# Two paired row blocks of five up tiles as seven block products instead of eight, with the loads of x spaced out

## The chip, the cores and the metric

The kernel runs on one core of a Trainium2 chip. The metric is the time of one execution in device microseconds (us), as the median of several runs. PE is TensorE (matmuls), PEld its weight loads, DVE is VectorE, ACT ScalarE, POOL GpSimd, and SP the engine whose queue issues most loads.

## The reference, cut to what matters

One layer of an encoder block in float32: 256 tokens (T), width 2048 (D, 16 row blocks of 128), feed-forward width 5632. Two attention mixers come first; then

```
gu = rms_norm(h, norm_pre_ffn) @ w_gate_up        # (256, 2048) x (2048, 11264)
g, up = gu[..., :5632], gu[..., 5632:]
h = h + rms_norm((silu(g) * up) @ w_down, norm_post_ffn)
```

The very first product, at the other place that the change touches, makes the latents: `u @ w_in` for the columns of q_lat (768) and kv_lat (512), where u is the normalised x.

## The kernel before, in words

**Products in three matmuls.** Every float32 product A B is done with A = Ah + Al and B = Bh + Bl, each half rounded to the matmul's float32r type: Ah Bh + Al Bh + Ah Bl. ACT makes the high half (a copy), DVE the low half (a subtraction), from raw weights that SP's queue loads. All this is one unit: a raw tile of 128 x 1024 (512 KB), and its hi and lo tiles. There are four buffers each of raw, hi and lo.

**The up product** (`up`, `two_products`, `up_unit`, line 805 on) goes over 11 tiles c. A tile makes 512 columns of g (side j = 0) and 512 of up (j = 1) for two token halves t of 128. For each of the 16 row blocks k there is one unit, and for each t and j three matmuls (lines 688 to 690) with 128 x 128 tokens as the stationary operand and 512 weight columns moving: 12 per unit, 192 per tile. The sums of (t, j) stand in PSUM: two buffers of two banks (`mm_pair`), one for each t. The first two units and the last two are ordered token half by token half, so that t = 0 ends 12 matmuls ahead of t = 1. `up_out` then makes silu(g) on ACT (line 861) and its product with up on DVE (line 863, tile ht); only then may the next tile write that buffer. Two units later PE transposes ht (`turn_split`, line 706) into one of four further banks (`at_bank`), from which ACT and DVE split it (lines 709, 710) into hid, which the down product reads.

**The first product** (`first_products`) goes over the 16 blocks k of x and, for each, three pairs p of latent blocks of q: 96 pairs of one 512 wide and one 256 wide matmul. Each k needs a block of x (`load_x`, `split_x`) and a unit of weights. Blocks 0 to 3 of x are loaded on SP's queue; after unit k, for k = 0 to 5, ACT's queue issues the load of blocks 2k + 4 and 2k + 5. When a pair of latents is done, its PSUM halves are added (lines 381, 382), one half j at a time with one tile tb for both; the kv product reuses the banks of the first pair.

**Order.** The kernel is written in Tile: a planner puts each engine's instructions into one order at build time, taking earlier lines of the program first among those that it reckons ready. Each engine then runs its list strictly in that order and waits at semaphores.

Of the kernel before, what the change touches and what calls it, by code (L numbers as in the profile page):

```python
# [10 lines left out]
F32 = mybir.dt.float32  # L11
# [3 lines left out]
ALU = mybir.AluOpType  # L15
# [39 lines left out]
def block_kernel(ctx: ExitStack, tc: tile.TileContext, a: dict, out: bass.AP):  # L55
# [11 lines left out]
    def slot(name, dt=F32):  # L67
        return sl.tile([P, 2, T], dt, tag="slot", name=name)
# [43 lines left out]
    def load_x(queue, k, n):  # L112
        if k % 2 == 0:
            xT[k // 2] = slot(f"xT{k // 2}")
        return queue.dma_start(xT[k // 2][:, k % 2:k % 2 + n], a["xT"][:, k:k + n, :]).ins

# [218 lines left out]
    def first_products():  # L335
# [7 lines left out]
        for k, p in order:  # L343
            if k not in w:
                if k < 3:
                    loaded = load_x(nc.sync, k, 1 if k < 2 else 2)
                with ExitStack() as held:
                    for ins in split_ins if k else ():
                        held.enter_context(tc.issue_after(ins.ins))
                    xsplit = split_x(k)  # L350
                with tc.issue_after(loaded), tc.issue_after(xsplit):
                    w[k] = unit("w_lat", 768, (256, 768) if k < 3 else None, (256, 768) if k == 0 else None)
                if 2 * k + 4 < KD:
                    with tc.issue_after(split_ins[0].ins):
                        load_x(S, 2 * k + 4, 2)
            hi, lo = w[k]
# [7 lines left out]
            if k == KD - 1:  # L364
                yield ps[p]

# [4 lines left out]
    for nm, n in (("q", 6), ("kv", 4)):  # L371
        acc = slot(f"acc_{nm}")[:, 0]
        g = cols[f"{nm}_norm"]
        for p in range(n // 2):
            s = tmp.tile([P, 2, T], F32, tag="t2", name="s", bufs=6)
            if nm == "kv":
                fold(pair(f"lat_{nm}{p}", "w_lat", KD, 4, xk), None, s)
            else:
                tb = tmp.tile([P, 2, T], F32, tag="t2", name="tb", bufs=6)
                for j, half in enumerate(next(q_products)):  # L380
                    S.activation(tb[:, j], half[:, T:], AF.Copy)
                    V.tensor_tensor(s[:, j], half[:, 0:T], tb[:, j], op=ALU.add)
            sq = tmp.tile([P, 2, T], F32, tag="t2", name="sq", bufs=6)
# [185 lines left out]
    def flat(t):  # L569
        return t.rearrange("p a b -> p (a b)")  # L570
# [230 lines left out]
    for t in range(2):  # L801
        for n in range(4):
            mg[t, n] = flat(slot(f"mg{t}{n}"))
    ahead = [[[flat(slot(f"{nm}_w_gu{k}{j}", F32R)) for j in range(2)] for nm in ("hi", "lo")] for k in range(AHEAD)]
    def up_unit(c, k):

        off = streams.get("w_gu", 0)
        streams["w_gu"] = off + P * 1024
        src = a["w_gu"][off:off + P * 1024].rearrange("(p c) -> p c", p=P)
        raw = wp.tile([P, 1024], F32, tag="raw", name=f"raw_w_gu_{off}", bufs=4)  # L810
        nc.sync.dma_start(raw, src)
        g = gf[:, k:k + 1]
# [46 lines left out]
    def up_out(ps, t, hts):  # L859
        s = tmp.tile([P, 512], F32, tag="t2", name="s", bufs=6)  # L860
        S.activation(s, ps[:, 0], AF.Silu, scale=r2s[t])
        ht = tmp.tile([P, 512], F32, tag="t2", name="ht", bufs=6)
        V.scalar_tensor_tensor(ht, ps[:, 1], r2s[t], s, op0=ALU.mult, op1=ALU.mult)  # L863
        hts.append(ht)

    def up(c):
# [17 lines left out]
    for c in range(KF // 4):  # L884
        up(c)

# [112 lines left out]
```

## Time and profile before

| | us |
|---|---|
| median of 3 runs (1383.34 to 1384.69) | 1383.67 |
| the profiled execution's own time | 1384.21 |
| its span, first to last instruction | 1382.5 |
| PE busy / DVE busy / ACT busy in the span | 1374.2 / 794.4 / 681.1 |

Busy time is what instructions took by their records; pipelined instructions of one engine overlap a little, so starts are the better measure of the pace. The own time of the profiled execution is 1.7 us more than the span, and 0.54 us more than the median.

### The profile page before, as it was taken

To read this page: it belongs to the slowest core of one execution; us is meant where nothing else is said; L and a number is where in the kernel's file an instruction comes from. 1 tells how busy PE (TensorE), PEld (TensorE's weight loads), DVE (VectorE), ACT (ScalarE), POOL (GpSimd) and SP (SyncE) were. 2 spreads that over 40 slices of the span, in tenths; PEclk is the share of its full clock that TensorE was granted. 3 is DMA by queue.
4 is the path that set the end of the run, shared out by engine and by line. 5 is a ranking of instruction groups with operands and counts; after the bars stand their busy time and mean duration, and the time that the engine had idled before them with its cause. 6 is when DMAs were issued, how large, how long until landed. Compare 5 with 4: busy or idle time off the path is not lost.

```text
span 1382.5 us, 16825 instructions
## 1 busy us (share of the span) xinstructions
PE 1374.2 (99%) x6414; PEld 1143.6 (83%) x6414; DVE 794.4 (57%) x921; ACT 681.1 (49%) x823; POOL 59.1 (4%) x95
## 2 busy tenths in 40 slices
PE   9999999999999999999999999999999999999998
PEld 8888888888888888888888888888888888888886
DVE  7996866555545566666545554555555545444444
ACT  6654444466558444555544444444444453434343
POOL 3310000000003100000000000000000001000000
PEclk9999999999999999999999999999999999999999
DMA  8655654565567655673666656565665666666663
GB/s 258 206 186 177 194 165 152 157 186 185 173 206 262 209 184 182 208 236 109 189 193 191 184 182 198 185 193 185 185 196 186 190 204 209 188 197 196 190 192 121
DMA packets 74545, 262.35 MB, mean 190 GB/s; under 512 B 8545, under 2 KB 9057, under 8 KB 74337
## 3 DMA queue, kind: packets, MB, share of 16 engines
q1 hardware_dynamic: 71424, 253.00, 58.8%
q0 software_dynamic: 1744, 6.29, 1.3%
q10 hardware_dynamic: 1296, 1.99, 0.4%
q8 instruction: 50, 0.82, 0.2%
q14 instruction: 31, 0.25, 0.0%
HBM read 259.15 MB, written 2.10 MB: 189 GB/s over the span
## 4 chain that ended last, share of the span: by engine, by line
PE 98%; DVE 1%; ACT 0%; issue 0%
PE gu_ps L688 12%; PE gu_ps L690 12%; PE gu_ps L689 12%; PE wd_ps L213 6%; PE wd_ps L215 6%; PE wd_ps L214 6%; PE gate_ps L213 4%; PE gate_ps L215 4%; PE gate_ps L214 4%; PE q_sb_ps L177 2%; PE k_sb_ps L177 2%; PE wout_ps L213 2%; PE wo_ps L690 2%; PE wout_ps L214 2%; PE wo_ps L688 2%; PE wo_ps L689 2%
## 5 line engine op out<-in xcount | busy, mean ns | idle before, releaser
L824 DVE SCALAR_TENSOR_TENSOR lo_w_gu<-raw_w_gu,packed,hi_w_gu 128x1024 fp32r<-128x1024 f32 x172 | 220.8, 1284 | 210.5 <-ACT hi_w_gu L823 208.9
L823 ACT ACTIVATE hi_w_gu<-raw_w_gu,packed 128x1024 fp32r<-128x1024 f32 x172 | 198.2, 1152 | 231.6 <-PE gu_ps L689 231.0
L688 PE MATMUL gu_ps<-hi_w_gu,hs 128*128 128x512 f32 x704 | 276.6, 393 | 0.0
L690 PE MATMUL gu_ps<-lo_w_gu,hs 128*128 128x512 f32 x704 | 275.3, 391 | 0.0
L689 PE MATMUL gu_ps<-hi_w_gu,hs 128*128 128x512 f32 x704 | 274.3, 390 | 0.0
L105 DVE TENSOR_TENSOR lo_w_down<-raw_w_down,hi_w_down 128x1024 fp32r<-128x1024 f32 x88 | 111.1, 1264 | 118.6 <-ACT hi_w_down L104 118.5
L104 ACT ACTIVATE hi_w_down<-raw_w_down 128x1024 fp32r<-128x1024 f32 x88 | 93.2, 1061 | 135.6 <-PE wd_ps L214 127.4
L688 PEld LDWEIGHTS gu_ps<-hi_w_gu,hs 128*128 128x128 f32 x704 | 132.2, 188 | 28.6 <-DVE ht L863 2.3
L690 PEld LDWEIGHTS gu_ps<-lo_w_gu,hs 128*128 128x128 f32 x704 | 132.2, 188 | 27.4
L689 PEld LDWEIGHTS gu_ps<-hi_w_gu,hs 128*128 128x128 f32 x704 | 132.2, 188 | 27.3 <-DVE hs L792 0.3
L105 DVE TENSOR_TENSOR lo_w_gate<-raw_w_gate,hi_w_gate 128x1024 fp32r<-128x1024 f32 x64 | 79.1, 1240 | 70.5 <-ACT hi_w_gate L104 64.3
L213 PE MATMUL gate_ps<-hi_w_gate,xs 128*128 128x512 f32 x256 | 100.6, 393 | 0.0
L215 PE MATMUL gate_ps<-lo_w_gate,xs 128*128 128x512 f32 x256 | 99.8, 390 | 0.0
L214 PE MATMUL gate_ps<-hi_w_gate,xs 128*128 128x512 f32 x256 | 99.6, 389 | 0.0
L104 ACT ACTIVATE hi_w_gate<-raw_w_gate 128x1024 fp32r<-128x1024 f32 x64 | 67.4, 1055 | 62.5 <-PE gate_ps L214 52.1
L104 ACT ACTIVATE hi_w_o<-raw_w_o 128x1024 fp32r<-128x1024 f32 x32 | 34.0, 1061 | 51.4 <-PE wo_ps L689 45.2
L105 DVE TENSOR_TENSOR lo_w_out<-raw_w_out,hi_w_out 128x1024 fp32r<-128x1024 f32 x32 | 39.2, 1225 | 33.6 <-ACT hi_w_out L104 33.4
L105 DVE TENSOR_TENSOR lo_w_o<-raw_w_o,hi_w_o 128x1024 fp32r<-128x1024 f32 x32 | 39.2, 1224 | 31.3 <-ACT hi_w_o L104 30.8
L215 PEld LDWEIGHTS gate_ps<-lo_w_gate,xs 128*128 128x128 f32 x256 | 48.1, 188 | 10.2
L214 PEld LDWEIGHTS gate_ps<-hi_w_gate,xs 128*128 128x128 f32 x256 | 48.1, 188 | 9.6
L213 PEld LDWEIGHTS gate_ps<-hi_w_gate,xs 128*128 128x128 f32 x256 | 48.1, 188 | 9.6
L104 ACT ACTIVATE hi_w_out<-raw_w_out 128x1024 fp32r<-128x1024 f32 x32 | 34.0, 1062 | 42.2 <-PE wout_ps L214 27.7
(452 smaller groups left out, 2541.8 us busy)
## 6 DMA issues: line engine op xcount, KB each, us to landing
raw_w_gu<-in_w_gu SPq DMA_DIRECT2D x176, 512.0 KB, 3.5
raw_w_down<-in_w_down SPq DMA_DIRECT2D x88, 512.0 KB, 4.2
raw_w_gate<-in_w_gate SPq DMA_DIRECT2D x64, 512.0 KB, 3.6
raw_w_o<-in_w_o SPq DMA_DIRECT2D x32, 512.0 KB, 3.7
raw_w_out<-in_w_out SPq DMA_DIRECT2D x32, 512.0 KB, 4.2
raw_w_q<-in_w_q SPq DMA_DIRECT2D x16, 512.0 KB, 3.8
raw_w_k<-in_w_k SPq DMA_DIRECT2D x16, 512.0 KB, 3.6
raw_w_v<-in_w_v SPq DMA_DIRECT2D x16, 512.0 KB, 3.5
```

The lines of the kernel that those rows point to most:

```text
L104: split_ins[0] = S.activation(hi[:, cs], raw[:, cs], AF.Copy)
L105: split_ins[1] = V.tensor_tensor(lo[:, cs], raw[:, cs], hi[:, cs].bitcast(F32), op=ALU.subtract)
L177: TE.matmul(ps[:, j, :], lhsT=hi[:, o:o + P], rhs=r, start=k == 0, stop=False, skip_group_check=True)
L213: TE.matmul(ps[t], lhsT=l[0][:, ts], rhs=hi[:, cs], start=k == 0, stop=False)
L214: TE.matmul(ps[t], lhsT=l[1][:, ts], rhs=hi[:, cs], start=False, stop=False)
L215: mm = TE.matmul(ps[t], lhsT=l[0][:, ts], rhs=lo[:, cs], start=False, stop=k == K - 1)
L688: TE.matmul(ps[t][:, j], lhsT=x[0][:, ts], rhs=hi[j], start=k == 0, stop=False)
L689: TE.matmul(ps[t][:, j], lhsT=x[1][:, ts], rhs=hi[j], start=False, stop=False)
L690: mm = TE.matmul(ps[t][:, j], lhsT=x[0][:, ts], rhs=lo[j], start=False, stop=k == K - 1)
L823: split_ins[0] = S.activation(hi, raw, AF.Copy, scale=g)
L824: split_ins[1] = V.scalar_tensor_tensor(lo, raw, g, hi.bitcast(F32), op0=ALU.mult, op1=ALU.subtract)
```

## The change

**Up tiles c = 1 to 5** run `up_fast`. In them the row blocks 8 and 10 form a pair, and 9 and 11 another. Before, a pair cost 2 blocks x 2 token halves x 2 sides = 8 products of a 128 x 128 by a 128 x 512 block, of three matmuls each. Now it costs seven (the scheme of Strassen in Winograd's form): 21 matmuls for 24.

- `token_sums`, once, makes the four sums of token blocks that the scheme needs, for both pairs, and splits them.
- `fast_pair` loads both raw units, lets ACT scale them in place by the norm's gain, and makes seven blocks of 128 x 512 from them, each split by a copy on ACT and a subtraction on DVE: three are as loaded, one (t3) is a difference of two of these, and three (T1, T2, T4) are a chain of differences in which each is made from the one before. The halves stand in tiles of the pool `sl`, not in the four hi and lo buffers.
- Three of the seven products go straight into the tile's PSUM sums. Four go to four banks of their own (q), over both pairs. They use all of `at_bank`'s four.
- At the step "collect", after the second pair, ACT copies one of the four banks and DVE makes four additions; at the end of the tile DVE adds the result to each of the four PSUM sums (four more), into SBUF tiles, on which `up_out` then works in place.
- The units of a tile stand in the order 0 to 3, pair, 4 to 7, pair, 12 to 15.

**The first product.** Blocks 4 and 5 of x are loaded after unit 0 as before, then blocks k + 3 and k + 4 after the units k = 3, 5, 7, 9, 11. Each load of two blocks is one contiguous stretch of memory. The first two pairs of latents are folded as whole pairs (`fold`); the third still goes by halves, with a tile tb for each.

```diff
+PAIRS = ((8, 10), (9, 11))
+FAST = range(1, 6)
...
-                if 2 * k + 4 < KD:
+                if k == 0 or k % 2 == 1 and 3 <= k < KD - 4:
                     with tc.issue_after(split_ins[0].ins):
-                        load_x(S, 2 * k + 4, 2)
+                        load_x(S, k + 3 if k else 4, 2)
...
             if k == KD - 1:
-                yield ps[p]
+                yield both[p] if p < 2 else ps[p]
...
+            elif p < 2:
+                fold(next(q_products), None, s)
             else:
-                tb = tmp.tile([P, 2, T], F32, tag="t2", name="tb", bufs=6)
                 for j, half in enumerate(next(q_products)):
-                    S.activation(tb[:, j], half[:, T:], AF.Copy)
-                    V.tensor_tensor(s[:, j], half[:, 0:T], tb[:, j], op=ALU.add)
+                    tb = tmp.tile([P, T], F32, tag="t2", name="tb", bufs=6)
+                    S.activation(tb, half[:, T:], AF.Copy)
+                    V.tensor_tensor(s[:, j], half[:, 0:T], tb, op=ALU.add)
...
     def up_out(ps, t, hts):
...
+        own = isinstance(ps, list)
+        gate, lin = ps if own else (ps[:, 0], ps[:, 1])
+        s = gate if own else tmp.tile([P, 512], F32, tag="t2", name="s", bufs=6)
+        S.activation(s, gate, AF.Silu, scale=r2s[t])
+        ht = lin if own else tmp.tile([P, 512], F32, tag="t2", name="ht", bufs=6)
+        V.scalar_tensor_tensor(ht, lin, r2s[t], s, op0=ALU.mult, op1=ALU.mult)
         hts.append(ht)
...
+    def token_sums():
...
+        def whole(o, k, t):
+            V.tensor_tensor(o, hs[:, k, 0, t].bitcast(F32), hs[:, k, 1, t].bitcast(F32), op=ALU.add)
...
+        V.tensor_tensor(s1, a21, a22, op=ALU.add)
+        V.tensor_tensor(s2, s1, a11, op=ALU.subtract)
+        V.tensor_tensor(s3, a11, a21, op=ALU.subtract)
+        V.tensor_tensor(s4, a12, s2, op=ALU.subtract)
...
+    def split_part(x, name):
+        hi, lo = flat(slot(f"{name}h", F32R)), flat(slot(f"{name}l", F32R))
+        split_ins[0] = S.activation(hi, x, AF.Copy)
+        split_ins[1] = V.tensor_tensor(lo, x, hi.bitcast(F32), op=ALU.subtract)
+        return hi, lo
...
+    def fast_pair(c, p, ps, q):
...
+        ra, rb = up_raw(c, ka), up_raw(c, kb)
+        for r, k in ((ra, ka), (rb, kb)):
+            S.activation(r, r, AF.Copy, scale=gf[:, k:k + 1])
+        (b11, b12), (b21, b22) = two_sides(ra), two_sides(rb)
...
+        product(q[0], rows(ka, 0), split_part(b11, f"fb11{c}{p}"), **ends)
+        product(ps[0][:, 0], rows(kb, 0), split_part(b21, f"fb21{c}{p}"))
+        product(ps[0][:, 1], sums[3, p], split_part(b22, f"fb22{c}{p}"))
+        t3 = flat(slot(f"ft3{c}{p}"))
+        V.tensor_tensor(t3, b22, b12, op=ALU.subtract)
+        V.tensor_tensor(b12, b12, b11, op=ALU.subtract)
+        product(q[3], sums[0, p], split_part(b12, f"ft1{c}{p}"), **ends)
+        product(q[2], sums[2, p], split_part(t3, f"fu3{c}{p}"), **ends)
+        V.tensor_tensor(b22, b22, b12, op=ALU.subtract)
+        product(q[1], sums[1, p], split_part(b22, f"ft2{c}{p}"), **ends)
+        V.tensor_tensor(b21, b21, b22, op=ALU.subtract)
+        return product(ps[1][:, 0], rows(kb, 1), split_part(b21, f"ft4{c}{p}"))
...
+        order = [(k, t) for t in range(2) for k in range(HEAD)] + [(2, 0), (2, 1), (3, 0), (3, 1), "pair0"]
+        order += [(k, t) for k in range(4, 8) for t in range(2)] + ["pair1", "collect"]
+        order += [(k, t) for k in (12, 13) for t in range(2)] + [(k, t) for t in range(2) for k in (14, 15)]
...
+            if step == "collect":
+                q1 = tmp.tile([P, 512], F32, tag="t2", name="q1", bufs=6)
+                S.activation(q1, q[0], AF.Copy)
+                add = [tmp.tile([P, 512], F32, tag="t2", name=f"q{i}", bufs=6) for i in range(3)]
+                V.tensor_tensor(add[0], q[1], q1, op=ALU.add)
+                V.tensor_tensor(add[1], q[2], add[0], op=ALU.add)
+                V.tensor_tensor(add[0], q[3], add[0], op=ALU.add)
+                V.tensor_tensor(add[2], q[3], add[1], op=ALU.add)
+                add = [[q1, add[0]], [add[1], add[2]]]
...
+            if k == KD - 1:
+                for j in range(2):
+                    V.tensor_tensor(add[t][j], ps[t][:, j], add[t][j], op=ALU.add)
+                up_out(add[t], t, hts)
...
-        up(c)
+        up_fast(c) if c in FAST else up(c)
```

## Rows read from the trace of the kernel before

**Rows 1.** The profile page of the whole execution: its first part (busy time of each engine and share of the span) and the engine sums of the chain that ended last.

```profile
PE 1374.2 (99%) x6414; PEld 1143.6 (83%) x6414; DVE 794.4 (57%) x921; ACT 681.1 (49%) x823; POOL 59.1 (4%) x95
...
PE 98%; DVE 1%; ACT 0%; issue 0%
```

**Rows 2.** All waits of PE over the whole span: waiter, line <- what released it: us in total, times, longest.

```profile
PE last L907 <- ACT diag L906: 1.7, 1, 1.7
PE warm L369 <- DVE ones L85: 1.1, 1, 1.1
PE lat_kv_ps L177 <- DVE s L382: 0.8, 1, 0.8
```

**Rows 3.** Waits from 660 to 1160 us, which holds the tiles c = 1 to 10 of the up product; same columns.

```profile
ACT hi_w_gu L823 <- PE gu_ps L689: 230.4, 166, 2.9
DVE lo_w_gu L824 <- ACT hi_w_gu L823: 208.9, 148, 2.7
...
PEld gu_ps L688 <- DVE ht L863: 2.3, 9, 0.3
```

**Rows 4.** Busy time of each engine in a stretch as long as one up tile (window, its length, then us busy and instructions of PE, PEld, DVE, ACT, POOL, granted clock, DMA share, GB/s).

```profile
730.15:774.75 44.60, 44.60 (x201) 36.74 (x200) 23.17 (x20) 20.65 (x21) 0.00 (x0) 1.00 0.61 189
```

**Rows 5.** Timeline of PE near the end of the tile c = 1 (start, us, engine, line, operation): two matmuls that stand twelve apart, and the first transposes of its hid. The tile's last matmul starts at about 732.2.

```profile
726.74 0.39 PE L688 MATMUL gu_ps<-hi_w_gu,hs 128*128 128x512 f32 x1
...
729.46 0.39 PE L688 MATMUL gu_ps<-hi_w_gu,hs 128*128 128x512 f32 x1
...
738.22 0.60 PE L706 MATMUL hid<-ident,ht 128*128 128x128 f32 x4
```

**Rows 6.** The page's costliest groups, those of the up tiles (busy us in all, mean ns of one | idle before them).

```profile
L824 DVE SCALAR_TENSOR_TENSOR lo_w_gu<-raw_w_gu,packed,hi_w_gu 128x1024 fp32r<-128x1024 f32 x172 | 220.8, 1284 | 210.5 <-ACT hi_w_gu L823 208.9
L823 ACT ACTIVATE hi_w_gu<-raw_w_gu,packed 128x1024 fp32r<-128x1024 f32 x172 | 198.2, 1152 | 231.6 <-PE gu_ps L689 231.0
...
L688 PEld LDWEIGHTS gu_ps<-hi_w_gu,hs 128*128 128x128 f32 x704 | 132.2, 188 | 28.6 <-DVE ht L863 2.3
```

**Rows 7.** Instructions that write or read the tile hid, for c = 1: shortest/median/longest ns, first and last start.

```profile
L709 ACT ACTIVATE hid1h<-hid x2: 578/578/579, 739.2 to 742.0; 128x512 fp32r<-128x512 f32 x2
L710 DVE TENSOR_TENSOR hid1l<-hid,hid1h x2: 683/684/684, 740.6 to 743.3; 128x512 fp32r<-128x512 f32 x2
```

**Rows 8.** Timeline of DVE in the projection stage, where it works without a gap.

```profile
147.36 0.68 DVE L187 TENSOR_TENSOR kn<-kn_ps,tb 128x512 f32<-128x512 f32 x1
147.96 0.41 DVE L409 TENSOR_TENSOR u<-s,trig 128x256 f32<-128x256 f32 x1
```

**Rows 9.** Timeline of DVE around the end of the tile c = 1.

```profile
725.18 1.28 DVE L824 SCALAR_TENSOR_TENSOR lo_w_gu<-raw_w_gu,packed,hi_w_gu 128x1024 fp32r<-128x1024 f32 x1 [1.44 <-ACT hi_w_gu L823]
...
730.38 0.75 DVE L863 SCALAR_TENSOR_TENSOR ht<-gu_ps,r2p,s 128x512 f32<-128x512 f32 x1 [1.20 <-ACT s L861]
731.98 2.64 DVE L824 SCALAR_TENSOR_TENSOR lo_w_gu<-raw_w_gu,packed,hi_w_gu 128x1024 fp32r<-128x1024 f32 x2 [0.85 <-ACT hi_w_gu L823]
734.54 0.75 DVE L863 SCALAR_TENSOR_TENSOR ht<-gu_ps,r2p,s 128x512 f32<-128x512 f32 x1
...
743.32 0.68 DVE L710 TENSOR_TENSOR hid1l<-hid,hid1h 128x512 fp32r<-128x512 f32 x1
```

**Rows 10.** The loads of raw weights: SP's queue at that place, and the page's line on them (KB each, median us from issue to landing).

```profile
726.49 8.49 SPq L811 DMA_DIRECT2D raw_w_gu<-in_w_gu  x4
...
raw_w_gu<-in_w_gu SPq DMA_DIRECT2D x176, 512.0 KB, 3.5
```

**Rows 11.** Busy time of each engine in two stretches in which DVE is busy nearly all the time; columns as in the tile's window.

```profile
80.00:100.00 20.00, 20.00 (x122) 17.65 (x121) 19.50 (x53) 13.33 (x18) 0.00 (x0) 1.00 0.53 162
...
140.00:160.00 20.00, 19.86 (x105) 16.79 (x104) 19.79 (x35) 9.20 (x12) 0.00 (x0) 1.00 0.45 142
```

**Rows 12.** Timeline of PE in the first product: its first matmul, the first of the seventh pair (one 512 wide, one 256 wide), two starts 21 pairs apart, and the first matmul of the next product.

```profile
4.55 0.77 PE L359 MATMUL lat_q_ps<-xs,hi_w_lat 128*128 128x512 f32 x1
...
8.03 0.39 PE L359 MATMUL lat_q_ps<-xs,hi_w_lat 128*128 128x512 f32 x1
...
28.64 0.39 PE L359 MATMUL lat_q_ps<-xs,hi_w_lat 128*128 128x512 f32 x1
...
35.92 0.39 PE L359 MATMUL lat_q_ps<-xs,hi_w_lat 128*128 128x512 f32 x1
...
41.39 0.47 PE L177 MATMUL lat_kv_ps<-xs,hi_w_lat 128*128 128x512 f32 x1 [0.80 <-DVE s L382]
```

**Rows 13.** Five of the first microseconds; columns as in the tile's window.

```profile
10.00:15.00 5.00, 5.00 (x29) 4.17 (x29) 3.41 (x6) 3.91 (x8) 0.00 (x0) 1.00 1.02 368
```

**Rows 14.** Waits in the first 45 us.

```profile
ACT hi_w_lat L104 <- DMA raw_w_lat<-in_w_lat: 6.4, 6, 1.9
...
ACT xs L119 <- DMA xT<-in_xT: 1.4, 2, 1.1
```

**Rows 15.** Timeline of DVE at the fold of the first latent pair.

```profile
39.95 0.42 DVE L382 TENSOR_TENSOR s<-lat_q_ps,tb 128x256 f32<-128x256 f32 x1
40.82 0.42 DVE L382 TENSOR_TENSOR s<-lat_q_ps,tb 128x256 f32<-128x256 f32 x1 [0.45 <-ACT tb L381]
```

**Rows 16.** Timeline of ACT there.

```profile
40.40 0.38 ACT L381 ACTIVATE tb<-lat_q_ps 128x256 f32<-128x256 f32 x1 [1.35 <-DVE s L382]
```

More of the change, by code (lines that the diff above doesn't have):

```diff
@@ L114, in load_x @@
             xT[k // 2] = slot(f"xT{k // 2}")
-        return queue.dma_start(xT[k // 2][:, k % 2:k % 2 + n], a["xT"][:, k:k + n, :]).ins
+        to = xT[k // 2][:, k % 2:k % 2 + n].rearrange("p a b -> p (a b)")
+        return queue.dma_start(to, a["xT"][k * P * T:(k + n) * P * T].rearrange("(p c) -> p c", p=P)).ins
     def split_x(k):
@@ L804, in block_kernel, with up_raw @@
     ahead = [[[flat(slot(f"{nm}_w_gu{k}{j}", F32R)) for j in range(2)] for nm in ("hi", "lo")] for k in range(AHEAD)]
-    def up_unit(c, k):
[L807 to L811, printed above, removed]
+    def up_raw(c, k):
+        off = (c * KD + k) * P * 1024
+        raw = wp.tile([P, 1024], F32, tag="raw", name=f"raw_w_gu_{off}", bufs=4)
+        nc.sync.dma_start(raw, a["w_gu"][off:off + P * 1024].rearrange("(p c) -> p c", p=P))
+        return raw
+    def up_unit(c, k):
+        raw = up_raw(c, k)
+        off = (c * KD + k) * P * 1024
         g = gf[:, k:k + 1]
@@ new lines, in split_part, with rows, product @@
+    def split_part(x, name):
[4 more added lines that the diff above has]
+    def fast_pair(c, p, ps, q):
+        ka, kb = PAIRS[p]
+        ra, rb = up_raw(c, ka), up_raw(c, kb)
+        for r, k in ((ra, ka), (rb, kb)):
+            S.activation(r, r, AF.Copy, scale=gf[:, k:k + 1])
+        (b11, b12), (b21, b22) = two_sides(ra), two_sides(rb)
+        def rows(k, t):
+            return hs[:, k, 0, t * P:t * P + P], hs[:, k, 1, t * P:t * P + P]
+        def product(to, x, w, start=False, stop=False):
+            TE.matmul(to, lhsT=x[0], rhs=w[0], start=start, stop=False)
+            TE.matmul(to, lhsT=x[1], rhs=w[0], start=False, stop=False)
+            return TE.matmul(to, lhsT=x[0], rhs=w[1], start=False, stop=stop)
+        ends = dict(start=p == 0, stop=p == len(PAIRS) - 1)
+        product(q[0], rows(ka, 0), split_part(b11, f"fb11{c}{p}"), **ends)
[10 more added lines that the diff above has]
+        return product(ps[1][:, 0], rows(kb, 1), split_part(b21, f"ft4{c}{p}"))
@@ new lines, in up_fast @@
+    def up_fast(c):
+        if not sums:
+            token_sums()
+        hts, ps, w, q = [], {}, {}, []
+        order = [(k, t) for t in range(2) for k in range(HEAD)] + [(2, 0), (2, 1), (3, 0), (3, 1), "pair0"]
+        order += [(k, t) for k in range(4, 8) for t in range(2)] + ["pair1", "collect"]
+        order += [(k, t) for k in (12, 13) for t in range(2)] + [(k, t) for t in range(2) for k in (14, 15)]
+        for step in order:
+            if step == "collect":
[7 more added lines that the diff above has]
+                add = [[q1, add[0]], [add[1], add[2]]]
+                continue
+            if isinstance(step, str):
+                p = int(step[-1])
+                if not q:
+                    q.extend(at_bank(f"q{c}{i}") for i in range(4))
+                mm = fast_pair(c, p, ps, q)
+                unit_done(mm)
+                unit_done(mm)
+                continue
+            k, t = step
+            if t not in ps:
+                ps[t] = mm_pair(f"gu{c}_ps{t}")
+            if k not in w:
+                w[k] = up_unit(c, k)
+            hi, lo = w[k]
+            x = [hs[:, k, i, t * P:t * P + P] for i in range(2)]
+            for j in range(2):
+                TE.matmul(ps[t][:, j], lhsT=x[0], rhs=hi[j], start=k == 0, stop=False)
+                TE.matmul(ps[t][:, j], lhsT=x[1], rhs=hi[j], start=False, stop=False)
+                mm = TE.matmul(ps[t][:, j], lhsT=x[0], rhs=lo[j], start=False, stop=k == KD - 1)
+            if t == 1:
+                unit_done(mm)
+            if k == KD - 1:
+                for j in range(2):
+                    V.tensor_tensor(add[t][j], ps[t][:, j], add[t][j], op=ALU.add)
+                up_out(add[t], t, hts)
+        for i in range(2):
+            at_unit(count[0] + 1 + i, lambda i=i: turn_split(hts, f"hid{c}", i, hid))
@@ L944, in _lay_out @@
     x2 = x.reshape(T, D)
+    xk = x2.T.reshape(KD, P, T)
     w = w_in[0]
```

25 lines of the change are left out of this document (20 added, 5 removed).

## The prediction

> **What bounds the kernel now.** I read the page first. PE is busy for 99% of the span and holds 98% of the chain that ended last, while DVE stands at 57% and ACT at 49% [rows 1]. Next all waits of PE: three in the whole span, 3.6 us together [rows 2]. So it is matmuls that set the end, and a matmul taken away is worth its place in PE's queue as long as nothing else gets late. Then the stage that is changed: in the up tiles ACT waits for PE to give back a hi buffer, and DVE waits for ACT [rows 3]; both are ahead of PE as far as the buffers let them. A stretch of one tile is 44.60 us with PE busy for all of it, DVE for 23.17 and ACT for 20.65; the granted clock is 1.00 and POOL does nothing [rows 4].
>
> **What a matmul is worth.** Twelve matmuls apart, starts stand 2.72 us apart [rows 5], so one takes 0.2267 us. The 0.39 us in its row are no price: the rows overlap.
>
> One rule of the Trainium skill speaks against this reading, and so against the change. "Perfetto Trace Analysis", section Identifying the Most-Contended Engine, says that matmul busy time doesn't show how near TensorE is to its limit, and that the busy share of weight loads does. Here that share is 83% [rows 1], and a load takes 188 ns [rows 6]; priced by loads, a removed matmul would be worth 0.188 us, the 30 of this change 5.6 us instead of 6.8. The spacing of starts decides, as the loads lie under the matmuls before them.
>
> **Removed from PE.** Each pair drops 3 of 24 matmuls; two pairs, five tiles: 30 matmuls x 0.2267 = **6.80 us**. Nothing is added to PE; the same 512 columns, the same loads. A fast tile should take 44.6 - 6 x 0.2267 = 43.25 us.
>
> **Added to DVE and ACT, per fast tile.** DVE loses four unit splits of 1.284 us (5.1) [rows 6]. It gains, 512 wide, 14 splits and 8 differences in the pairs, 4 additions in collect and 4 at the tile's end: 30 x 0.684 [rows 7] = 20.5 us. That is 23.2 - 5.1 + 20.5 = 38.6 us of 43.25, or 89%; by starts it is less, since such instructions follow each other every 0.60 us [rows 8]: 30 x 0.60 = 18.0, 36 us, 83%. ACT loses four copies of 1.152 us and gains four of the same (the scaling in place), 14 copies of 0.58 and one more: 20.7 + 8.7 = 29.4 us, 68%. Both engines fit on the average, so the question is whether the pair's work comes in time.
>
> **Does it come in time?** Call the end of the previous tile on PE 0 (732.4 in the trace for c = 1). Four units and the transposes take 4 x 2.72 + 0.9, so PE reaches the first pair at 11.8, its seven products start 0.68 us apart, and the last one (the end of the chain T1, T2, T4) starts at 15.9. The loads: the raw buffer for the pair's first block comes free with the low half of the next tile's first unit, made at 725.18 to 726.46 [rows 9]; SP issues the load at once, at 726.49, and it lands 3.5 us later in the median [rows 10]. The second follows at -3.2 and lands at about +0.5. From 0.5 to 15.9, 15.4 us, DVE owes: the two late unit splits (2.6), two additions and the product ht of the late token half (1.4 + 0.75), the two splits of hid (1.4), the eleven instructions of the pair (7.5, or 6.6 by starts) and the next unit's split (1.3): 14.9 us by durations, 13.3 by starts. So there is cover of 0.5 to 2.1 us at the last product, and more at the first, which wants one split alone. The chain's links (0.68 for the difference, 0.58 for the copy, 0.68 for the subtraction, 1.94 us) hold DVE only for 1.36 of that, and others fill the rest. The units 4 to 7 need hi buffers that are free from 4.1 us on, and are wanted at 16.6 at the earliest. The second pair has 10.9 us of units ahead of it in which DVE owes three splits (3.9) and its own 7.5; its loads queue on SP behind those of units 6 and 7, which wait for the first pair's raw buffers. I cost all that at **0**; without the cover, each microsecond that a pair is late costs ten.
>
> Is such a load on DVE borne? The nearest rows say so: from 80 to 100 us DVE is busy for 19.50 of 20 and PE for 20.00; from 140 to 160 DVE has 19.79 and PE 19.86 [rows 11]. The bounds for lost time on PE are so 0 and 0.14 per 20 us: 0 to 1.5 us for five tiles. I take 0, by the row that is busier on PE's side and as a fast tile asks less of DVE.
>
> **The end of a tile.** Before, a PSUM buffer comes free after silu and ht (0.75); now after two additions (1.2 to 1.4), with no ACT between, and silu and ht follow in SBUF. The late half has 2.72 us. Today that wait already takes PE's load 2.3 us over nine times [rows 3]; I put the change at 0, between -0.1 and +0.5 per tile. The four banks of q want both hid transposes read, the later at 743.32 + 0.68 [rows 9], which is 11.6, ahead of the first write to the third bank (13.2). The one-off sums for tokens (eight 256 wide at 0.41 [rows 8], two splits) are 4.7 us of DVE in the tile c = 0, where it idles 1.44 us before each unit split [rows 9]: 0.
>
> **The first product.** Its first matmul starts at 4.55 us and the next product at 41.39 [rows 12]. 21 pairs of one wide and one narrow matmul take 7.28 us, 0.347 each; all 96 would take 33.3, so 3.56 us are lost. Of these, 1.40 lie ahead of the seventh pair at 8.03, which took 3.48 us for 2.08; the first load of x that is moved was issued at about 7.4, so these stay. 0.80 are the wait for the fold [rows 2]. The rest, 1.36, is gaps while the loads of x share the DMA engines with the weights (busy share 1.02 from 10 to 15 us [rows 13]; ACT waits 6.4 us for weights but 1.4 for x [rows 14]). Spacing the loads can give back 0 to 1.36. It can also make x late: a load issued after the split of unit k serves unit k + 3, 6.2 us of PE later; the longest wait for x now is 1.1 us, so I bound the loss by that, once. I take **-0.4**, nearer to nothing, since the weights wait for buffers as well. The fold: DVE adds the first half at 39.95 and the second at 40.82 [rows 15], because ACT's second copy waits at 40.40 for the first addition [rows 16]. One copy and one addition of 512 would end at 39.95 + 0.68 in place of 41.24: **-0.6**, bounds -0.8 and 0.
>
> **Sum.** -6.8 - 0.4 - 0.6 = -7.8 us. On the profiled execution, 1384.21 - 7.8 = 1376.4; the median lies 0.54 below it, so **1375.9**.
>
> **The rivals.**
> - *DVE runs short in the pairs.* The cover above is 0.5 us in the worse count. If the planner places unit splits ahead of the pair's, or a load lands late, each pair stalls PE by 0.4 to 0.8 us and most of the gain goes: 1380 to 1384, say 1382. For it: 89% by durations, and a strict order per engine. Against it: [rows 11].
> - *The chain lies open: slower.* If the pair's work starts only when PE stands before it (a raw buffer freed late, or an in-order queue in which ACT's copy of a T waits behind a copy for a unit whose buffer PE holds), each of three links costs 1.94 us against 0.68 of matmuls, 1.26 x 3 = 3.8 us per pair, 38 in all: 1414. In part it decides from 0.78 us per pair on, where the gain is gone, and by 1.05 us the kernel is slower by over 0.2%. Against it: the loads land 11 us ahead.
> - *Late x.* The spaced loads cost 1.1 instead of giving 0.4: 1377.4.
> - *The change doesn't do what it says.* If the planner's order leaves the saved matmuls as holes, or the count of PE doesn't fall by 30: only the first product's part stays, 1382.7.
>
> **How the numbers follow.** The forecast (1374.4 to 1378) has 0.72, late x 0.08, DVE short 0.11, the open chain 0.07, no effect 0.02. About 0.2% (2.8 us) is what a measurement of this kernel can tell from no change. Faster takes the forecast, late x and 0.03 of DVE short: 0.83; same 0.10 (0.08 and 0.02); slower 0.07. The range runs from 1374.4 (1383.67 - 6.8 - 1.36 - 0.8, and 0.3 for the tile ends) to 1381, so that it takes in the bounds of 1.5 us for DVE and of late x, and the better part of DVE short, and leaves out some 0.17.
>
> **What would show it.** PE's instructions: 6384 for 6414. Tiles c = 1 to 5: 43.25 us apart instead of 44.6, PE without waits for the products of the pairs, DVE at 36 to 39 us per tile. In the first product the next one starts at about 40.4, with no wait for the fold. The forecast is wrong if the waits of PE list splits of the pairs, if the additions at a tile's end come behind unit splits in DVE's order, or if ACT waits for x.

## The result, and the profile after

| | us |
|---|---|
| changed kernel, median of 8 runs (1387.13 to 1390.84) | 1388.38 |
| kernel before, median of 8 runs (1383.32 to 1385.11) | 1383.83 |
| ratio, with 95% interval | 1.0032 (1.0023 to 1.0041) |
| span of the profiled execution | 1386.6 |

The forecast was 1375.9, faster; the kernel became slower by 0.3%, and 1388.4 lies above the range. From the page, the busy times of part one and the chain that ended last (the same lines of before are [rows 1]):

```profile
PE 1373.4 (99%) x6384; PEld 1134.2 (82%) x6384; DVE 859.3 (62%) x1059; ACT 718.6 (52%) x898; POOL 58.8 (4%) x95
...
PE 84%; DVE 6%; DMA 5%; ACT 3%; issue 1%; SPq 0%; ACTq 0%
```

The 30 matmuls are gone (6384 for 6414), yet the chain now runs through DVE, DMA and ACT for 14% of the span, where PE alone had 98%. "99% busy" hides it: a matmul's record is 0.39 us long at starts 0.23 us apart, so the figure covers small holes. The waits say more. First those of PE from 680 to 920 us, which holds the five fast tiles (there were none there before), then those of ACT for loads in the same stretch (before, ACT waited there for PE only [rows 3]): us in total, times, longest. PE's twelve waits there, of which five are shown, come to 4.9 us.

```profile
PE q L929 <- ACT fb1110h L912: 0.9, 1, 0.9
PE q L931 <- DVE fb1120l L913: 0.8, 1, 0.8
PE gu_ps L929 <- ACT ft431h L912: 0.4, 1, 0.4
PE q L931 <- DVE fb1140l L913: 0.4, 1, 0.4
...
PE gu_ps L931 <- DVE ft421l L913: 0.2, 1, 0.2
```

```profile
ACT hi_w_gu L831 <- DMA raw_w_gu<-in_w_gu: 21.7, 22, 2.0
...
ACT raw_w_gu L922 <- DMA raw_w_gu<-in_w_gu: 12.8, 9, 2.4
```

PE waits for the first split of a first pair (fb11) and for the last one of a second pair (ft4, of T4). The halves of a block are named by it, by c, by the pair's number (0 or 1), and h (high) or l (low). A wait's own figure is less than what it costs, as the starts around it show (PE in tile c = 2):

```profile
743.91 0.39 PE L930 MATMUL q<-fb1120h,hs 128*128 128x512 f32 x1
745.05 0.50 PE L931 MATMUL q<-fb1120l,hs 128*128 128x512 f32 x1 [0.76 <-DVE fb1120l L913]
745.39 0.40 PE L929 MATMUL gu_ps<-fb2120h,hs 128*128 128x512 f32 x1
```

```profile
765.00 0.47 PE L931 MATMUL q<-ft221l,sum_h 128*128 128x512 f32 x1
765.87 0.49 PE L929 MATMUL gu_ps<-ft421h,hs 128*128 128x512 f32 x1 [0.40 <-ACT ft421h L912]
766.20 0.39 PE L930 MATMUL gu_ps<-ft421h,hs 128*128 128x512 f32 x1
...
767.27 0.50 PE L931 MATMUL gu_ps<-ft421l,hs 128*128 128x512 f32 x1 [0.21 <-DVE ft421l L913]
767.61 0.40 PE L984 MATMUL gu_ps<-lo_w_gu,hs 128*128 128x512 f32 x1
```

From 743.91 to 745.05 is 1.14 us where 0.23 was due: 0.91 lost for a wait of 0.76, and the next start is 0.34 behind, 0.11 more. The first transposes of hid, one set for each tile, start at 691.82, 737.26, 783.52, 829.58, 875.42 and 920.43: 45.4, 46.3, 46.1, 45.8 and 45.0 us apart, 228.6 in all, where 43.25 each (216.3) was forecast and the five stretches took 223.6 before. So the tiles lose 12.3 us of stalls against a gain of 6.8. The stretch behind them belongs to the change too: it takes 45.08 us, and 44.62 before, so the tiles are 5.5 us slower in all. One tile as a whole (columns as in [rows 4]) has the load that was forecast for DVE and ACT:

```profile
737.62:783.88 46.26, 44.78 (x198) 35.03 (x196) 35.99 (x46) 28.27 (x35) 0.00 (x0) 1.00 0.58 183
```

The late first split comes from ACT's order (start, duration, what it made, in brackets the idle time before it):

```profile
734.39 1.14 ACT L922 ACTIVATE raw_w_gu<-raw_w_gu,packed 128x1024 f32<-128x1024 f32 x1
737.90 0.60 ACT L714 ACTIVATE hid1h<-hid 128x512 fp32r<-128x512 f32 x1 [2.37 <-PE hid L711]
738.53 1.15 ACT L831 ACTIVATE hi_w_gu<-raw_w_gu,packed 128x1024 fp32r<-128x1024 f32 x1
741.33 1.16 ACT L831 ACTIVATE hi_w_gu<-raw_w_gu,packed 128x1024 fp32r<-128x1024 f32 x1 [1.64 <-DMA raw_w_gu<-in_w_gu]
742.38 0.57 ACT L714 ACTIVATE hid1h<-hid 128x512 fp32r<-128x512 f32 x1
742.86 0.62 ACT L912 ACTIVATE fb1120h<-raw_w_gu 128x512 fp32r<-128x512 f32 x1
```

Both raw blocks are scaled at 735.5. ACT then stands idle 2.4 us for hid, splits units 4 and 5, stands 1.6 us for a load, and comes to the pair's first split at 742.86, right behind the second split of hid. In all five first pairs of the built order fb11 stands behind that second hid, in four of them directly.

The head gained what was forecast, in this execution. Kv's first matmul starts at 39.99 in place of 41.39 [rows 12], and one copy (37.98) and one addition of 512 do the fold [rows 15, 16]:

```profile
39.99 0.50 PE L180 MATMUL lat_kv_ps<-xs,hi_w_lat 128*128 128x512 f32 x1
```

```profile
39.25 0.68 DVE L190 TENSOR_TENSOR s<-lat_q_ps,tb 128x512 f32<-128x512 f32 x1
```

This place varies: in the traces of the runs below that have the same head, that matmul starts at 39.65 to 41.40, and in three of them (e4, e5, e12) PE waits for the fold again, 0.5 to 0.9 us. ACT's waits for x grew in the changed kernel, from 1.4 us [rows 14] to 4.0 in four times.

### The profile page after: what moved, and what is told of

Same layout as the page of the kernel before. It is cut to its first block, busy times and chain, and to the rows that moved or that the text cites. A ratio compares the mean times of both kernels' runs of the same rounds, so it can differ in the third digit from the quotient of the medians.

```text
span 1386.6 us, 16964 instructions
## 1 busy us (share of the span) xinstructions
PE 1373.4 (99%) x6384; PEld 1134.2 (82%) x6384; DVE 859.3 (62%) x1059; ACT 718.6 (52%) x898; POOL 58.8 (4%) x95
## 4 chain that ended last, share of the span: by engine, by line
PE 84%; DVE 6%; DMA 5%; ACT 3%; issue 1%; SPq 0%; ACTq 0%
PE gu_ps L694 6%; PE gu_ps L693 6%; PE gu_ps L695 6%; PE wd_ps L216 6%; PE wd_ps L218 6%; PE wd_ps L217 6%; DMA raw_w_gu<-in_w_gu 4%; PE gate_ps L218 4%; PE gate_ps L216 4%; PE gate_ps L217 4%; DVE lo_w_gu L832 2%; PE k_sb_ps L180 2%; PE q_sb_ps L180 2%; PE wout_ps L216 2%; PE wo_ps L695 2%; PE wout_ps L218 2%
## 5 line engine op out<-in xcount | busy, mean ns | idle before, releaser
L832 DVE SCALAR_TENSOR_TENSOR lo_w_gu<-raw_w_gu,packed,hi_w_gu 128x1024 fp32r<-128x1024 f32 x152 | 194.9, 1283 | 128.3 <-ACT hi_w_gu L831 127.4
L831 ACT ACTIVATE hi_w_gu<-raw_w_gu,packed 128x1024 fp32r<-128x1024 f32 x152 | 174.3, 1150 | 163.7 <-PE gu_ps L694 117.9
L693 PE MATMUL gu_ps<-hi_w_gu,hs 128*128 128x512 f32 x384 | 151.0, 393 | 0.0
L695 PE MATMUL gu_ps<-lo_w_gu,hs 128*128 128x512 f32 x384 | 150.1, 391 | 0.0
L694 PE MATMUL gu_ps<-hi_w_gu,hs 128*128 128x512 f32 x384 | 149.7, 390 | 0.0
L982 PE MATMUL gu_ps<-hi_w_gu,hs 128*128 128x512 f32 x240 | 94.6, 394 | 0.0
L984 PE MATMUL gu_ps<-lo_w_gu,hs 128*128 128x512 f32 x240 | 93.7, 391 | 0.0
L983 PE MATMUL gu_ps<-hi_w_gu,hs 128*128 128x512 f32 x240 | 93.6, 390 | 0.0
L693 PEld LDWEIGHTS gu_ps<-hi_w_gu,hs 128*128 128x128 f32 x384 | 72.1, 188 | 15.5 <-DVE ht L874 1.0
L694 PEld LDWEIGHTS gu_ps<-hi_w_gu,hs 128*128 128x128 f32 x384 | 72.1, 188 | 14.9 <-DVE hs L797 0.3
L695 PEld LDWEIGHTS gu_ps<-lo_w_gu,hs 128*128 128x128 f32 x384 | 72.1, 188 | 14.9
```

The source lines that it names most:

```text
L693: TE.matmul(ps[t][:, j], lhsT=x[0][:, ts], rhs=hi[j], start=k == 0, stop=False)
L694: TE.matmul(ps[t][:, j], lhsT=x[1][:, ts], rhs=hi[j], start=False, stop=False)
L695: mm = TE.matmul(ps[t][:, j], lhsT=x[0][:, ts], rhs=lo[j], start=False, stop=k == K - 1)
L831: split_ins[0] = S.activation(hi, raw, AF.Copy, scale=g)
L832: split_ins[1] = V.scalar_tensor_tensor(lo, raw, g, hi.bitcast(F32), op0=ALU.mult, op1=ALU.subtract)
L982: TE.matmul(ps[t][:, j], lhsT=x[0], rhs=hi[j], start=k == 0, stop=False)
```

## The experiments

Three theories. **A, the place in the pool:** the pair's split tiles come from the pool `sl`, behind hid's, and ACT's order puts the splits only where the planner has a place for them, long after the blocks landed. **B, the raw buffers:** a pair holds two of four of them till the end of its sums (first block until T1 is split, second until T4 is), so the units' loads come late. **C, load:** DVE and ACT have too much to do in these tiles, wherever it is put. In the table, "pool" means new split tiles for every use and "kept" tiles taken once and used by every pair; "zeros" is an early first write of the kept tiles, and "early sums" moves `token_sums` into the tile c = 0. The column of stretches is the sum of the five, transposes to transposes, in the profiled execution. The runs were made in groups, each with runs of the kernel before beside it, whose median lay between 1383.8 and 1384.3.

| run | split tiles of the pair | raw blocks held | zeros | early sums | us | ratio (95% interval) | five stretches |
|---|---|---|---|---|---|---|---|
| changed kernel | pool | yes | | | 1388.4 | 1.0032 (1.0023 to 1.0041) | 228.6 |
| e1, head alone | (none) | | | | 1383.2 | 0.9991 (0.9982 to 0.9999) | 223.5 |
| e2, tiles alone | pool | yes | | | 1391.2 | 1.0048 (1.0035 to 1.0061) | 229.9 |
| e3 | kept | yes | | | 1387.6 | 1.0021 (1.0012 to 1.0031) | 226.1 |
| e5 | pool | no | | | 1392.7 | 1.0056 (1.0042 to 1.0070) | 232.4 |
| e4 | kept | no | | | 1383.6 | 0.9993 (0.9985 to 1.0002) | 224.6 |
| e6 | pool | yes | | yes | 1387.6 | 1.0026 (1.0017 to 1.0036) | 227.3 |
| e7 | kept | no | | yes | 1381.1 | 0.9977 (0.9968 to 0.9985) | 220.3 |
| e8 | kept | no | yes | yes | 1375.9 | 0.9940 (0.9926 to 0.9954) | 215.9 |
| e12 | kept | no | yes | | 1375.4 | 0.9941 (0.9927 to 0.9954) | 216.5 |
| e9 | kept | yes | yes | yes | 1386.9 | 1.0012 (1.0002 to 1.0022) | 226.1 |
| e10, six tiles | kept | yes | yes | yes | 1386.6 | 1.0015 (1.0007 to 1.0024) | 225.4 |
| e11 | kept | yes, by a reader | yes | yes | 1386.5 | 1.0020 (1.0011 to 1.0029) | 226.8 |

**e1 and e2, the two parts.** e1 has `FAST = range(0)`; e2 has the head of before.

> The changed head (paced loads of x, whole-pair folds of kv and of the first two query pairs) alone, all up tiles as before. If the trace of after is read rightly (the first tile of the up product began 1.2 us sooner than before and nothing else of the head moved): 1382.6 us, 1.2 below before. If the pacing itself costs what makes the changed kernel slower: 1386 to 1388 us, 2 to 4 above before.

> The two pairs in five tiles alone, the head as before. If the loss sits in the tiles (fast tiles 45.9 us apart on average where 43.26 was forecast): 1389.6 us, 1.2 above the changed kernel, since the head's gain is gone. If the head is what costs: 1380 to 1383 us, below before. The two parts should add: the sum of this difference and that of the head alone is that of the whole change.

Measured: 1.1 us below before (1384.28) and 6.9 above. The sum, 5.8, is near the 4.6 of the whole; in e2's first fast tile PE also ran some 3 us at the lower clock (see the end), which the changed kernel's trace does not have. The head is not what costs; the loss is in the tiles.

**e3, e4 and e5: kept tiles, free raw buffers.** e3:

```diff
+        own.extend([flat(slot(f"own{i}", F32R)) for i in range(14)] + [flat(slot("own_t3"))])
...
-        hi, lo = flat(slot(f"{name}h", F32R)), flat(slot(f"{name}l", F32R))
+        i = ("fb11", "fb21", "fb22", "ft1", "fu3", "ft2", "ft4").index(name[:-2])
+        hi, lo = own[2 * i], own[2 * i + 1]
```

e4 has besides, and e5 alone, four more such tiles for the scaled halves:

```diff
-        for r, k in ((ra, ka), (rb, kb)):
-            S.activation(r, r, AF.Copy, scale=gf[:, k:k + 1])
-        (b11, b12), (b21, b22) = two_sides(ra), two_sides(rb)
+        b11, b12, b21, b22 = [x.bitcast(F32) for x in own[15:]]
+        for r, k, sides in ((ra, ka, (b11, b12)), (rb, kb, (b21, b22))):
+            for j in range(2):
+                S.activation(sides[j], r[:, j * 512:j * 512 + 512], AF.Copy, scale=gf[:, k:k + 1])
```

> As the changed kernel, but the pair's fourteen split tiles and the difference t3 are taken from the pool once and used again by every pair, so that they no longer queue in the pool behind the tiles of the hidden row that is turned and split beside them. Theory A (the pair's splits wait for their turn in the pool, behind the second split of hid of the tile before): ACT then splits the first pair's raw blocks ahead of that second hid, and the gaps of TensorE at the first pair (1.30, 1.14, 0.75, 0.78, 0.44 us and about 0.5 us at T1) go: 5 tiles x 1 to 1.5 us, 1381 to 1384 us; the gap ahead of the last product of the second pair (1.3 us a tile with its restart) may stay. Theory B (two of the four raw buffers are held by the pair, so loads come late): the splits still come late, waiting for DMA, 1387 to 1389 us. Theory C (DVE and ACT together have too much to do in these tiles): the first pair's gaps only move to a later product, 1386 to 1389 us.

> As the run with tiles of its own, and ACT writes the four scaled halves of a pair into four further tiles of its own in place of writing them back over the raw blocks: the raw buffers come free 2.5 us after they landed and not at the end of the pair's sums (some 10 us later). Theory A alone: no more than 0.5 us below the run with tiles of its own. Theory B: the loads of units 4 to 7 and of the second pair come earlier, ACT's waits for raw blocks (21.7 and 12.8 us in this stage of the changed kernel) fall under 10 us, and the gaps ahead of the second pair's last product go: 5 x 1.3 us, 1376 to 1378 us. Theory C: the gaps stay, ACT's load grows by 10 x 2 fixed costs of an operation, 0.5 us slower at most than the run with tiles of its own.

> The changed kernel with four tiles of its own for the scaled halves alone, so that raw buffers come free early, but with the pair's split tiles still taken from the pool for every pair. It completes a square of four with the changed kernel (1388.4), tiles of its own for the splits (1387.6) and both (1383.6). Theory A with B as two separate sums: 4 us below the changed kernel, 1384.4. Theory A needed before B can show (the splits must first be able to come early): 1387 to 1389 us. Theory B alone (the pool's order is beside the point): 1383 to 1384 us.

The medians are 1387.6, 1383.6 and 1392.7, and the runs of e3 lie far apart (1381.8 to 1389.8). The first median suits B or C; the other two suit no theory. The stretches say why. In e3 they are 47.2, 47.5, 43.5, 43.5 and 44.4 us. In e4 they are 51.4, 43.4, 43.2, 43.2 and 43.4 us: four tiles as forecast, and a first one 8 us too long. In e5 they are 50.7, 44.9, 45.4, 46.1 and 45.3. So against e5 kept split tiles are worth 2.1 us in each of the later four, which speaks for A, and a mean over five tiles had hidden it. Free raw buffers alone (e5) make the later four 1.5 us shorter in sum than in the changed kernel and the first 5.3 longer. What the first tile loses, PE of e4 shows:

```profile
698.28 0.39 PE L987 MATMUL gu_ps<-lo_w_gu,hs 128*128 128x512 f32 x1
702.43 0.50 PE L932 MATMUL q<-own,hs 128*128 128x512 f32 x1 [3.76 <-ACT own L914]
...
709.40 0.63 PE L987 MATMUL gu_ps<-lo_w_gu,hs 128*128 128x512 f32 x1
709.83 0.63 PE L985 MATMUL gu_ps<-hi_w_gu,hs 128*128 128x512 f32 x1
...
710.63 0.40 PE L932 MATMUL q<-own,sum_h 128*128 128x512 f32 x1
710.86 0.39 PE L933 MATMUL q<-own,sum_l 128*128 128x512 f32 x1
```

PE stands for 3.8 us, and then starts come 0.43 us apart instead of 0.23 until 710.6: the clock has gone to its lower level. In e5's first tile the same happens behind a wait of 3.7 us, and in e3 in each of the first two stretches, so these medians hold a stall and a lower clock behind it.

**e6 and e7, the token sums earlier.** They move to unit 10 of the tile c = 0. The edit is made to the changed kernel in e6 and to e4 in e7:

```diff
-             (1, 2): [(turned, 0, 2)], (1, 3): [(turned, 1, 2)], (1, 4): [(turned, 0, 3)], (1, 5): [(turned, 1, 3)]}
+             (1, 2): [(turned, 0, 2)], (1, 3): [(turned, 1, 2)], (1, 4): [(turned, 0, 3)], (1, 5): [(turned, 1, 3)], (0, 10): [(token_sums,)]}
```

> The changed kernel with the token sums (eight additions and two splits) put into the second half of the tile ahead of the first fast one, ahead of unit 10 there; nothing else. In the trace of the changed kernel they run at 688 to 694 us, between the first splits of the first fast tile, whose first pair then stalls 1.3 us more than that of the third. Expected: that tile gets some 1 to 2 us shorter, the others stay: 1386.5 to 1387.5 us. If the sums' place is beside the point: 1388 us.

> Split tiles of its own, raw buffers freed early, and the token sums in the tile ahead. With own tiles and free raw buffers the later four fast tiles stood 43.2 to 43.4 us apart, as forecast for the whole change, and only the first took 51.4 us: ACT waited 2.2 us for the sums between the first unit splits, the pair's raw blocks were scaled at 699.3 and not ahead of 698, TensorE stood for 3.8 us and then ran 17 matmuls at half the clock. With the sums out of the way the first tile should be as the others: 1383.6 less some 7 us, 1376 to 1378 us, which is the forecast for the change (1375.9). If the first tile's stall has another cause (the loads of the pair themselves late): 1381 to 1384 us.

e6 is 0.8 us below the changed kernel, which is not clear of noise (the intervals overlap), though its first stretch is 44.2 us (45.4 in the changed kernel). e7 gained 2.5 on e4, not 7: its first stretch is still 47.4, the other four 43.2 to 43.4. ACT in that first tile of e7:

```profile
686.89 1.14 ACT L831 ACTIVATE hi_w_gu<-raw_w_gu,packed 128x1024 fp32r<-128x1024 f32 x1
690.81 1.15 ACT L831 ACTIVATE hi_w_gu<-raw_w_gu,packed 128x1024 fp32r<-128x1024 f32 x1 [2.77 <-DMA raw_w_gu<-in_w_gu]
...
695.39 0.60 ACT L714 ACTIVATE hid0h<-hid 128x512 fp32r<-128x512 f32 x1 [0.76 <-PE hid L711]
695.89 2.55 ACT L926 ACTIVATE own<-raw_w_gu,packed 128x512 f32<-128x512 f32 x4
```

The pair's loads were issued at 680.42 and 683.14 and landed 3.5 us later, by 686.6. ACT scales them at 695.89, again behind the second hid, after 2.8 us of idling for unit 4. It is theory A's picture once more, now at the first write of kept tiles.

**e8 and e12, zeros.** If a tile has its place from its first write on, a first write long before should free the pair. The zeros are no part of the computation. In e8's trace GpSimd writes them between 578 and 638 us, in nine spells, each behind a wait for DVE or PE.

```diff
+        for t in own:
+            G.memset(t.bitcast(F32), 0.0)
```

For e8, which is e7 with this edit, it stands in `token_sums`; e12 has it, with the taking of the tiles, in a function of its own that is called at (0, 10), and calls `token_sums` from `up_fast` again.

> As the run with tiles of its own, raw buffers freed early and early sums; besides, GpSimd writes zeros once into the nineteen kept tiles in the second half of the tile ahead of the first fast one (the zeros are overwritten, so nothing of the result changes). This tests theory A at the one tile where it was left: there the kept tiles are written for the first time, and so get their place in the pool in that tile; ACT scaled the first pair's raw blocks at 695.9, behind both splits of hid and two units, though they had landed at 683.9 and 686.6. If a place in the pool is what the pair waits for, the zeros take that place early, ACT scales right behind the split of unit 3 (688 us), the stall of some 4.3 us in the first tile goes, all five fast tiles stand 43.2 to 43.4 us apart, and the time is 1381.1 less 4.3: 1376 to 1377.5 us. If the first tile's stall has another cause (loads): unchanged at 1380 to 1381.5 us. The zeros could also cost: GpSimd works beside DVE there; DVE has some 12 of 30 us idle, so no more than 1 us.

> As the run with free raw buffers and zeros written early (1375.9), but the token sums stay at the start of the first fast tile, as in the changed kernel; only the places of the kept tiles are taken early. If the early sums matter by themselves (DVE and ACT are busy with them at 688 to 694 us, ahead of that tile's first pair): 1.5 to 4 us above it, 1377.5 to 1380 us. If only the places matter: 1376 us.

e8: 1375.94, stretches of 43.1 to 43.2 us. All waits of PE in its whole span, ACT in the first tile, and a tile's window and its ends on PE:

```profile
PE last L1040 <- ACT diag L1039: 1.7, 1, 1.7
PE warm L372 <- DVE ones L87: 1.1, 1, 1.1
PE lat_q_ps L362 <- ACT hi_w_lat L106: 0.8, 2, 0.4
```

```profile
686.71 1.14 ACT L831 ACTIVATE hi_w_gu<-raw_w_gu,packed 128x1024 fp32r<-128x1024 f32 x1
687.75 2.56 ACT L928 ACTIVATE own<-raw_w_gu,packed 128x512 f32<-128x512 f32 x4
690.20 2.19 ACT L916 ACTIVATE own<-own 128x512 fp32r<-128x512 f32 x4
692.29 0.59 ACT L714 ACTIVATE hid0h<-hid 128x512 fp32r<-128x512 f32 x1
```

```profile
734.50:777.69 43.19, 43.19 (x196) 35.61 (x194) 35.70 (x48) 28.50 (x40) 0.00 (x0) 1.00 0.59 195
```

```profile
734.50 0.60 PE L711 MATMUL hid<-ident,q 128*128 128x128 f32 x4
```

ACT scales at once and splits the pair ahead of hid. DVE is as busy as in the changed kernel (35.7 us of a tile against 36.0), and in the fast tiles PE waits for nothing: theory C has fallen. e12 leaves the sums where the changed kernel has them, and is no slower (1375.4): what I expected of early sums was wrong. If they matter, it is only as long as the pair comes late (e6, e7).

**e9, e10 and e11: raw blocks held again.** e9 is e8 with the scaling in place (fifteen kept tiles); e10 is e9 with `FAST = range(1, 7)`. Scaling in place holds a raw buffer and also ties ACT's and DVE's order, so e11 parts the two: it is e8 with a late reader of the raw block.

```diff
+        for r, x in ((ra, own[7]), (rb, own[13])):
+            keep = const.tile([P, 1], F32, tag="keep", name="keep", bufs=2)
+            G.tensor_tensor(keep, r[:, 0:1], x[:, 0:1].bitcast(F32), op=ALU.add)
```

> The same with raw blocks scaled in place as in the changed kernel (raw buffers held by the pair to the end of its sums); fifteen kept tiles, zeros written early, early sums. It asks whether the raw buffers (theory B) matter once theory A's stall is gone in every tile. If they do: the second pair's last product and the first pair's third still stall as in the run with tiles of its own (0.4 to 1.3 us a tile): 1379 to 1382 us. If not: as the run with free raw buffers, 1376 to 1377.5 us.

> The run before with a sixth fast tile (the pool has room for it as no tiles for scaled halves are held): six matmuls of 0.2267 us fewer, 1.36 us below the run before if the added tile has no stalls, 0 to 0.5 below it if the stalls of the raw buffers are in it too.

> As the run with free raw buffers and zeros written early (1375.9), but GpSimd adds one column of each raw block of a pair to one column of the last split that the block's numbers go into (the split of T1 for the first block, of T4 for the second), into a tile that nobody reads. So a raw buffer is held as long as in the changed kernel, while the scaled halves stay in tiles of their own and ACT, DVE and TensorE have the same work. If what the in-place scaling costs is the raw buffers (theory B): 1383 to 1388 us, ACT waits for raw blocks of 40 us or more between 680 and 920 us. If it is the order that writing in place forces on ACT and DVE: 1376 to 1377.5 us.

e9 is 10.9 us above e8 and e11 10.6; e10 is no faster than e9 (0.3 below by the medians, above by the ratios). Held raw buffers cost all of it here, by whatever they are held. They need not cost it in every tile: e3 holds them too, and its tiles c = 3 and c = 4, behind a stall of 2.2 us and a lower clock, took 43.5 us each, while its five stretches came to the same 226.1 us as those of e9. Whether the stall had let the loads get ahead was not tried. SP's queue from 680 to 920 us, what the loads waited for, in e8 and then in e11:

```profile
SPq L813 <- DVE lo_w_gu L832: 183.7, 62, 7.1
SPq L813 <- ACT own L928: 19.6, 20, 1.7
```

```profile
SPq L813 <- DVE lo_w_gu L832: 130.3, 57, 7.2
SPq L813 <- POOL keep L953: 66.9, 20, 8.7
```

ACT's waits for loads grow from 14.3 us (14.0 and 0.3) in e8 to 59.9 in e11:

```profile
ACT hi_w_gu L831 <- DMA raw_w_gu<-in_w_gu: 35.5, 25, 3.8
...
ACT own L928 <- DMA raw_w_gu<-in_w_gu: 24.4, 11, 4.6
```

And how a late unit reaches PE, in e11's tile c = 2: ACT, then PE.

```profile
739.95 1.16 ACT L831 ACTIVATE hi_w_gu<-raw_w_gu,packed 128x1024 fp32r<-128x1024 f32 x1 [1.03 <-DMA raw_w_gu<-in_w_gu]
...
743.65 0.64 ACT L916 ACTIVATE own<-own 128x512 fp32r<-128x512 f32 x1 [1.54 <-DVE own L947]
...
746.05 0.63 ACT L916 ACTIVATE own<-own 128x512 fp32r<-128x512 f32 x1 [0.72 <-DVE own L949]
```

```profile
746.74 0.50 PE L934 MATMUL gu_ps<-own,hs 128*128 128x512 f32 x1 [0.76 <-ACT own L916]
```

A unit's split, waiting for its load, stands in ACT's and DVE's lists ahead of the chain's last links. The unit is not wanted yet; T2 and T4 behind it are. T4 then comes late to PE, though the first product of that pair was in time.

## Why the prediction was wrong

By its own steps:

- **What a matmul is worth (0.2267 us): right.** With the stalls gone (e8), the last four stretches are 43.16 to 43.22 us where the kernel before has 44.61 to 44.62: 1.43 less, of which six matmuls are 1.36. The section Identifying the Most-Contended Engine of the Trainium skill's "Perfetto Trace Analysis" judges TensorE's headroom by MFU, the share of its peak, and the busy share of weight loads; priced by weight loads, which is the prediction's own step from there, the six were worth 1.13. The trace decides for the spacing. Nor was the rest of that share headroom: in a tile without waits before, weight loads were busy for 36.74 of 44.60 us [rows 4], and e8 is faster at the same 83% over the whole span.
- **The load on DVE and ACT: right.** 36.0 and 28.3 us per tile measured, 36 to 38.6 and 29.4 forecast. That such a load is borne, which I argued from [rows 11], e8 confirms (35.7 and 28.5, and no wait of PE).
- **"Does it come in time?", costed at 0: the step that failed,** twice. It let the pair begin when its blocks land, and added up what DVE owes between there and the last product, in any order. ACT's list decides, not the sum: the first split came 7.3 us after the blocks were scaled (735.53 to 742.86), and ahead of it ACT stood idle for hid and for a unit's load. I had counted raw buffers, hi buffers and banks, but not the pool of the split tiles: with tiles kept and written early (e8) the same split comes ahead of hid. And I saw that units 6 and 7 and the second pair wait for the first pair's raw buffers, and priced that at 0, since those units are wanted late. What is wanted late still stood ahead of what is wanted soon in an in-order list. Together they cost 12.4 to 13 us (1388.4 against 1375.9 in e8 and 1375.4 in e12, which leaves the sums in their place). Neither alone gives it back: kept tiles written early (e9) 1.5 us by the medians, 2.8 by the ratios; free raw buffers alone (e5) none, as what they gave in four tiles was lost in the first.
- **The tile's end (0, from -0.1 to +0.5): right** in e8 (the 0.07 that is left of the 1.43). With raw blocks held it is not: in e9 PE waits 2.4 us, in three times, for the additions at the end, and 1.4 of them come when ACT has stood 4.7 us for the next pair's load, ahead of silu in its list.
- **Token sums at 0, in the idle time of the tile c = 0: wrong place, right price.** They ran at 688 to 694 us, in c = 1. What that cost with the pair late is not clear of noise (0.8 us, e6); e12 shows no cost.
- **The head (-0.4 and -0.6): right in the sum.** -1.1 us by e1; 1.4 at kv's first matmul in the one execution. No run parts the two terms, and ACT's waits for x, named as a sign of being wrong, did grow (1.4 to 4.0 us) without that showing in the time.
- **The rivals.** The one that said "DVE runs short" was wrong in its cause. "The chain lies open: slower" came nearest: it named a raw buffer freed late and a copy in an in-order queue behind one for a unit. It did not name the place in the pool, and the unit in front waited for its load, not for a buffer that PE holds. Its turning point held: I put slower from 1.05 us per pair on, and ten pairs lost 1.2 each. It had 0.07; against it stood only that the loads land early, which is no answer to a place in a list.
- **The range.** Its lower end takes 0.3 us for the tile ends, where -0.1 per tile makes 0.5; the measured time lies beyond the other end.

The sum put right, in us: -6.8 for matmuls, -1.1 for the head, +12.3 of stalls by the stretches is +4.4; measured +4.6. The forecast time was that of e8 and e12.

What stays open: why the planner put the pair's first writes behind the second hid. That a first write long before takes them out from there is shown (e7 against e8, 5.1 us); that what they lacked was a place in the pool is the theory behind that edit, and how the planner hands out places was not looked at. More than four raw buffers were not tried.

## What to carry to other kernels

When a step makes its own operands just ahead of their use, ask three things apart: when its inputs land, whether its output tiles have a place by then, and what stands before it in each in-order list. A sum of busy time over the stretch answers none of these. In this kernel a tile that is used again and again was better taken once, and written once, long before its first hurry. And a buffer of a small ring that is worked on in place is held for the whole chain; a copy out of it (at no cost that shows here, ACT was at 66%) gives it back at once.

## What was not expected of the hardware

- A stall can cost twice. In e4 PE stood for 3.8 us, and the granted clock then was 0.62 in the mean of nine microseconds, so that for the most of them TensorE ran at the lower of its two levels (1.2 for 2.4 GHz). Window, length, and columns as in [rows 4]:

```profile
702.00:711.00 9.00, 8.06 (x19) 5.45 (x20) 7.80 (x12) 6.16 (x11) 0.00 (x0) 0.62 0.69 235
```

  From 703.99 to 710.63 us 14 matmuls start in 6.64 us where 3.17 were due; 0.18 of the rest is a wait, so some 3 us came on top of the stall. Three other traces show it too: behind waits of 1.2 and 0.4 us (e2), of 1.3 and 0.4 and later of 1.8 (e3), and of 3.7 (e5), the granted clock was 0.56 to 0.64 in the mean of the 3.5 to 9 us behind. In e9 and e11, with single waits of 1.4 us, and in the changed kernel, with waits of up to 0.9, it stayed at 1.00 in the fast tiles.
- A restart of PE after a wait costs some 0.1 us more than the wait shows: the next start comes 0.33 to 0.34 us later instead of 0.23 (745.05 to 745.39, 765.87 to 766.20 and 767.27 to 767.61).
